# A macaron decoder layer on one core: the feed-forwards' exchange transfers issued by GpSimd, and one PSUM bank for the last quarter of the second down product

## The chip, the core and the metric

The kernel runs on one core of a Trainium2 chip, in one launch. The metric is the device time of a run in microseconds (us); three runs of the kernel before are known, and one more execution was taken with the hardware profiler. Engines are named as in the profile: PE is TensorE's matmul, PEld its weight load, DVE is VectorE, ACT is ScalarE, POOL is GpSimd, SP is SyncE, which here only issues transfers.

## The reference

One decoder layer on 256 tokens of width 1024, all in float32:

```python
h = h + 0.5 * swiglu(rms_norm(h, ffn1_norm), ffn1_w_gate, ffn1_w_up, ffn1_w_down)
h = h + hybrid_mixer(rms_norm(h, mix_norm), ...)     # two kinds of attention, gated, merged
h = h + 0.5 * swiglu(rms_norm(h, ffn2_norm), ffn2_w_gate, ffn2_w_up, ffn2_w_down)
out = rms_norm(h, final_norm)

def swiglu(x, w_gate, w_up, w_down):
    return (jax.nn.silu(x @ w_gate) * (x @ w_up)) @ w_down     # 1024 -> 2816 -> 1024
```

The change touches the two feed-forwards (swiglu) only.

## The kernel before

**Arithmetic.** Every product of float32 matrices is made of three matmuls on high and low parts: `mm3` issues a_high x w_high, a_high x w_low and a_low x w_high into one PSUM accumulation (lines 287, 288, 289). `unit` is one `mm3`, one step of the weave and one chance to prepare a weight tile.

**Weights.** All weights lie in HBM as one stream of 376 tiles of 128 x 512, in the order of their use. SP loads them in chunks of two tiles (512 KB, line 144) into three `raw` buffers; a chunk is issued when the third chunk before it has been split up. `Weights.split` makes a tile's parts: ACT writes the high part (`wh`, line 158 with the norm's gain, 155 without), DVE the low part (`wl`, line 159 or 156). `pump` lets this run up to 7 tiles ahead of the tile in use, in ten buffers.

**Order of the work.** PE and SP run in the order in which the program is written. For ACT, DVE and POOL a planner, which simulates the program at build time, sets the order of instructions, but for the first blocks of the first feed-forward and the end of the second one, where the written order holds (`ordered`). The weave is a list of generators: a generator that yields n goes on after n more units. So a constant such as `D_MOVED` sets where in the written order a step is put.

**A feed-forward** (`ffn`). The hidden width of 2816 is taken in 11 blocks b of 256. A block has 8 weight tiles, each with gate and up columns side by side, and two tiles t of 128 tokens: 16 units. After each of the two, `hidden` makes silu (ACT, line 397), the product (DVE, line 398) and a DVE transpose of 32 x 32 squares into `hs` (line 406). The transpose leaves each square in its place in the 4 x 4 grid, so `exchange` moves square (i, j) to (j, i) by 16 transfers from SBUF to SBUF (line 421, `hm` <- `hs`), one written after each unit, on SP's queue, for two blocks at once (six exchanges in a feed-forward, the last for one block). 14 steps behind, `split` makes the high and low parts `hth`, `htl` of the result (lines 308, 309), which the down product takes as its stationary side.

**The down product** goes over 22 rows k of 128 of the hidden width, two halves c of the output columns and two token tiles t, into four PSUM accumulations. The first 18 rows (the head) run with all four in turn; the last four (`TAIL`) are taken by one (t, c) after the other, so that each half is ready as early as it can be. In the second feed-forward the quarter (t, c) = (1, 1) is kept in two pieces of 256 columns in two PSUM banks over all 22 rows, so that the final norm can begin on the first piece while the second is still being accumulated. `residual` (line 486) adds half of a bank to h.

Other work on POOL: constants and a norm's Newton steps at the beginning, the same steps after the first feed-forward, rotary and mask work in the mixer, four transfers `bg` (line 834) and one `gB` (line 917).

The first feed-forward also carries `rope_tables` (lines 535 to 589), a chain of small DVE instructions for the rotary tables, which enters the weave at unit 100.

Of the kernel before, what the change touches and what calls it, by code (L numbers as in the profile page):

```python
# [23 lines left out]
KF = FF // P  # L24
# [11 lines left out]
WB = 10  # L36

D_TURNED = 3
D_MOVED = 14
D_TURN = 10  # L40
D_READY = 7
D_NORM0 = 9
# [141 lines left out]
def hybrid_layer_kernel(ctx, tc, x, xt, pos, g_final, bgate, wstream, out):  # L184
    nc = tc.nc
# [9 lines left out]
    def acc_bank(nm):  # L195
        return psum.tile([P, 512], F32, name=nm, tag="acc", bufs=3)

    def y_bank(nm):
        return psum.tile([P, 512], F32, name=nm, tag="y", bufs=1)

    def two_banks(nm):
        return psum.tile([P, 1024], F32, name=nm, tag="pr", bufs=2)

    def big(nm, dt=F32R):
        return work.tile([P, 1024], dt, name=nm, tag="big", bufs=24)

    def wide(nm, w=768):
        return work.tile([P, w], F32, name=nm, tag="f", bufs=4)
# [76 lines left out]
    def mm3(o, ah, al, w, first, last):  # L285
        wh, wl = w
        nc.tensor.matmul(o, ah, wh, start=first, stop=False)  # L287
        nc.tensor.matmul(o, ah, wl, start=False, stop=False)  # L288
        nc.tensor.matmul(o, al, wh, start=False, stop=last)  # L289

    def unit(o, a, w, first, last):
        mm3(o, a[0], a[1], w, first, last)
        weave.tick()
        W.pump()

    def unit_pair(os, blocks, w, first, last):

        wh, wl = w
        for o, (ah, al) in zip(os, blocks):
            nc.tensor.matmul(o, ah, wh, start=first, stop=False)  # L300
            nc.tensor.matmul(o, al, wh, start=False, stop=False)
        for o, (ah, al) in zip(os, blocks):
            nc.tensor.matmul(o, ah, wl, start=False, stop=last)
            weave.tick()
            W.pump()

    def split(dst_h, dst_l, src, hi_engine=None, rest=nc.vector):
        (hi_engine or nc.scalar.copy)(dst_h, src)
        rest.tensor_sub(dst_l, src, dst_h.bitcast(F32))
# [66 lines left out]
    def lagged(n, lag):  # L376

        for k in range(n + lag):
            if k < n:
                yield 0, k  # L380
            if k >= lag:
                yield 1, k - lag


    def ffn(base, xn, nm, on_half, lag, last=False):


        hts = {}
        squares = {}

        def slots(q):

            return q.rearrange("p (s w) -> p s w", w=P)

        def hidden(b, t, bank):
            sh = wide(f"sh_{nm}{b}_{t}", 512)
            silu = nc.scalar.activation(sh[:, 0:256], bank[:, 0:256], AF.Silu, scale=xn[t].r)
            prod = nc.vector.scalar_tensor_tensor(sh[:, 256:512], bank[:, 256:512], xn[t].r, sh[:, 0:256],
                                                  op0=ALU.mult, op1=ALU.mult)
            marks["silu"], marks["prod"] = silu.ins, prod.ins  # L400

            p = b // 2
            if p not in squares:
                squares[p] = big(f"hs_{nm}{b}", F32)
            dst = slots(squares[p])[:, b % 2 * 4 + t:b % 2 * 4 + t + 3:2]
            nc.vector.transpose(dst, sh[:, 256:512].rearrange("p (c w) -> p c w", w=P))
            if t == 1 and (b % 2 or b == FB - 1):
                weave.add(exchange(p, b % 2 * 4 + 4), D_TURNED)

        def later(f, *args):  # L410
            f(*args)
            return
            yield

        def exchange(p, n):

            moved = big(f"hm_{nm}{p}", F32)
            w = 32
            for i in range(4):
                for j in range(4):  # L420
                    nc.sync.dma_start(slots(moved)[j * w:j * w + w, 0:n, i * w:i * w + w],  # L421
                                      slots(squares[p])[i * w:i * w + w, 0:n, j * w:j * w + w])
                    yield 1
            yield D_MOVED
            hts[p] = big(f"hth_{nm}{p}"), big(f"htl_{nm}{p}")
            split(hts[p][0][:, 0:n * P], hts[p][1][:, 0:n * P], moved[:, 0:n * P])

        for b in range(FB):
            if b == 1:
                W.ahead = AHEAD  # L430
            if b == 2:
                ordered.close()
            banks = {}
            if b == 0 and lag == 0:
                pair = two_banks(f"gu_{nm}0")
                banks = {t: pair[:, t * 512:t * 512 + 512] for t in range(2)}
                for k in range(KD):
                    unit_pair([banks[t] for t in range(2)], [xn[t].blk(k) for t in range(2)], W.get(base + k),
                              k == 0, k == KD - 1)
                    W.done(base + k)  # L440
                for t in range(2):
                    weave.add(later(hidden, b, t, banks[t]), D_FIRST[t])
            for t, k in lagged(KD, 2 if b else lag) if b or lag else ():
                if k == 0:
                    banks[t] = acc_bank(f"gu_{nm}{b}_{t}")
                i = base + b * KD + k
                unit(banks[t], xn[t].blk(k), W.get(i), k == 0, k == KD - 1)
                if t == 1:
                    W.done(i)
                if k == KD - 1:  # L450
                    weave.add(later(hidden, b, t, banks[t]), 0 if b else D_FIRST[t])

        base += FB * KD
        banks = {}

        def out_bank(t, c):
            if (t, c) not in banks:
                if (t, c) != (1, 1):
                    banks[t, c] = acc_bank(f"dn_{nm}{t}{c}")
                else:  # L460
                    banks[t, c] = y_bank(f"dn_{nm}{t}{c}")
                    if last:
                        banks[t, c] = banks[t, c], two_banks(f"dn_{nm}{t}{c}b")
            return banks[t, c]

        def down(t, c, k, i, piece=None):

            o = k % 4 * 256 + t * P
            ht = [q[:, o:o + P] for q in hts[k // 4]]
            w = W.get(i)  # L470
            bank = out_bank(t, c)
            if (t, c) == (1, 1) and last:
                for j in range(2) if piece is None else (piece,):
                    mm3(bank[j][:, 0:256], *ht, [q[:, j * 256:j * 256 + 256] for q in w], k == 0, k == KF - 1)
                weave.tick()
                W.pump()
            else:
                unit(bank, ht, w, k == 0, k == KF - 1)

        def residual(t, c, piece=None):  # L480
            if piece is None:
                ps, s = banks[t, c][:, 0:512], slice(c * 512, c * 512 + 512)
            else:
                ps = banks[t, c][piece][:, 0:256]
                s = slice(c * 512 + piece * 256, c * 512 + piece * 256 + 256)
            nc.vector.scalar_tensor_tensor(h[t][:, s], ps, 0.5, h[t][:, s], op0=ALU.mult, op1=ALU.add)

        head = KF - TAIL
        for k in range(head):
            for c in range(2):  # L490
                for t in range(2):
                    down(t, c, k, base + 2 * k + c)
                W.done(base + 2 * k + c)
        weave.flush()
        if last:
            ordered.enter_context(tc.manual_schedule())
        for t in range(2):
            for c in range(2):
                pieces = (0, 1) if last and (t, c) == (1, 1) else (None,)
                for piece in pieces:  # L500
                    for k in range(head, KF):
                        i = base + 2 * head + c * TAIL + k - head
                        down(t, c, k, i, piece)
                        if t == 1 and piece in (None, 1):
                            W.done(i)
                    residual(t, c, piece)
                    on_half(t, c, piece)
# [87 lines left out]
    def next_norm(dst, nm):  # L595
# [12 lines left out]
        return on_half  # L608

    ffn(0, xn, "f1", next_norm(un, "u"), 0)  # L610
    with tc.issue_after(marks["silu"]):
        nc.scalar.preload_act_table_set("natural_log_exp_and_others")
# [192 lines left out]
    a, b, ys = {}, {}, {}  # L805
# [47 lines left out]
    for c in range(2):  # L853
        banks = {}
        for t, k in lagged(4, 2):
            if k == 0:
                banks[t] = acc_bank(f"ba{t}{c}")
            i = W_BR + c * 4 + k
# [28 lines left out]
    for t in range(2):  # L887
        for c in range(2):
            ps = acc_bank(f"bb{t}{c}")
            for k in range(4):  # L890
                i = W_BR + 8 + c * 4 + k
# [8 lines left out]
    for c in range(2):  # L900
        s = slice(c * 512, c * 512 + 512)
        for t in range(2):
            if (t, c) == (1, 0):
                weave.flush()
            ps = acc_bank(f"wo{t}{c}")
            for k in range(KD):
                i = W_OUT + c * KD + k
# [100 lines left out]
```

## Time and profile before

| | |
|---|---|
| median of 3 runs | 571.09 us (569.05 to 572.18) |
| the profiled execution | 569.89 us, of which span 568.0 us |
| mean granted TensorE clock | 0.994 |
| busy share of the span | PE 98%, PEld 80%, DVE 70%, ACT 60%, POOL 8% |
| chain that ended last | PE 84%, DMA 7%, DVE 4%, ACT 2% |

The span runs from the first to the last instruction of the execution. Busy shares count instructions, not waits or issues of transfers; the chain of work that ended last is followed back from the last instruction to what released each step.

### The profile page before, as it was taken

To read this page: it belongs to the slowest core of one execution; us is meant where nothing else is said; L and a number is where in the kernel's file an instruction comes from. 1 tells how busy PE (TensorE), PEld (TensorE's weight loads), DVE (VectorE), ACT (ScalarE), POOL (GpSimd) and SP (SyncE) were. 2 spreads that over 40 slices of the span, in tenths; PEclk is the share of its full clock that TensorE was granted. 3 is DMA by queue.
4 is the path that set the end of the run, shared out by engine and by line. 5 is a ranking of instruction groups with operands and counts; after the bars stand their busy time and mean duration, and the time that the engine had idled before them with its cause. 6 is when DMAs were issued, how large, how long until landed. Compare 5 with 4: busy or idle time off the path is not lost.

```text
span 568.0 us, 7807 instructions
## 1 busy us (share of the span) xinstructions
PE 555.2 (98%) x2580; PEld 456.2 (80%) x2580; DVE 395.0 (70%) x685; ACT 338.3 (60%) x576; POOL 43.5 (8%) x93
## 2 busy tenths in 40 slices
PE   9999989999999999999999999999999999999995
PEld 5778868778888888888888888788888878788884
DVE  6777595866466766879897878766667757754655
ACT  6855454755355666767867755466555655553643
POOL 1200000000000436000021200040000000000000
PEclk9999989999999999999999999999999999999998
DMA  8946757867687466433544564555667777786741
GB/s 299 399 101 202 188 176 194 231 194 202 171 292 255 148 199 217 159 137 112 185 134 162 185 198 148 181 176 188 181 191 213 213 203 206 206 194 195 248 156 74
DMA packets 78007, 109.57 MB, mean 193 GB/s; under 512 B 51600, under 2 KB 51856, under 8 KB 77968
## 3 DMA queue, kind: packets, MB, share of 16 engines
q1 hardware_dynamic: 77072, 106.85, 61.4%
q0 software_dynamic: 464, 1.57, 0.8%
q10 hardware_dynamic: 432, 0.67, 0.3%
q8 instruction: 20, 0.33, 0.2%
q14 instruction: 19, 0.16, 0.1%
HBM read 102.25 MB, written 1.05 MB: 182 GB/s over the span
## 4 chain that ended last, share of the span: by engine, by line
PE 84%; DMA 7%; DVE 4%; ACT 2%; issue 1%; SPq 1%; ACTq 0%
PE gu_f L288 11%; PE gu_f L289 10%; PE gu_f L287 10%; PE dn_f L287 7%; PE dn_f L288 7%; PE dn_f L289 7%; DMA raw<-in_wstream 6%; PE in L287 6%; PE in L288 6%; PE in L289 6%; DVE wl L159 2%; PE wo L287 1%; PE wo L289 1%; PE wo L288 1%; SPq L421 1%
## 5 line engine op out<-in xcount | busy, mean ns | idle before, releaser
L158 ACT ACTIVATE wh<-raw,first 128x512 fp32r<-128x512 f32 x256 | 173.6, 718 | 81.8 <-DMA raw<-in_wstream 51.5
L159 DVE SCALAR_TENSOR_TENSOR wl<-raw,first,wh 128x512 fp32r<-128x512 f32 x256 | 182.8, 748 | 56.2 <-ACT wh L158 55.5
L156 DVE TENSOR_TENSOR wl<-raw,wh 128x512 fp32r<-128x512 f32 x120 | 78.4, 690 | 43.9 <-ACT wh L155 43.5
L155 ACT CAST wh<-raw 128x512 fp32r<-128x512 f32 x120 | 69.5, 619 | 60.6 <-DMA raw<-in_wstream 43.9
L288 PE MATMUL gu_f<-wl,zh 128*128 128x512 f32 x176 | 68.7, 390 | 1.0 <-DVE wl L159 1.0
L287 PE MATMUL gu_f<-wh,zh 128*128 128x512 f32 x176 | 68.7, 391 | 0.0
L289 PE MATMUL gu_f<-wh,zl 128*128 128x512 f32 x176 | 68.5, 389 | 0.0
L288 PE MATMUL gu_f<-wl,xh 128*128 128x512 f32 x160 | 63.5, 397 | 3.2 <-DVE wl L159 2.9
L287 PE MATMUL dn_f<-wh,hth_f 128*128 128x512 f32 (+1 forms) x176 | 66.5, 378 | 0.0
L288 PE MATMUL dn_f<-wl,hth_f 128*128 128x512 f32 (+1 forms) x176 | 66.3, 377 | 0.0
L289 PE MATMUL dn_f<-wh,htl_f 128*128 128x512 f32 (+1 forms) x176 | 66.2, 376 | 0.0
L287 PE MATMUL in<-wh,uh 128*128 128x512 f32 x160 | 63.8, 399 | 0.0
L287 PE MATMUL gu_f<-wh,xh 128*128 128x512 f32 x160 | 63.5, 397 | 0.2 <-ACT wh L158 0.2
L289 PE MATMUL gu_f<-wh,xl 128*128 128x512 f32 x160 | 62.8, 393 | 0.0
L289 PE MATMUL in<-wh,ul 128*128 128x512 f32 x160 | 62.5, 391 | 0.0
L288 PE MATMUL in<-wl,uh 128*128 128x512 f32 x160 | 62.5, 391 | 0.0
L288 PEld LDWEIGHTS gu_f<-wl,zh 128*128 128x128 f32 x176 | 33.0, 188 | 8.4 <-DVE wl L159 1.7
L288 PEld LDWEIGHTS gu_f<-wl,xh 128*128 128x128 f32 x160 | 30.4, 190 | 10.8 <-DVE wl L159 3.9
L287 PEld LDWEIGHTS gu_f<-wh,zh 128*128 128x128 f32 x176 | 33.0, 188 | 7.3 <-ACT wh L158 0.5
L289 PEld LDWEIGHTS gu_f<-wh,zl 128*128 128x128 f32 x176 | 33.0, 188 | 6.8
L287 PEld LDWEIGHTS dn_f<-wh,hth_f 128*128 128x128 f32 x176 | 33.1, 188 | 6.4
L289 PEld LDWEIGHTS dn_f<-wh,htl_f 128*128 128x128 f32 x176 | 33.1, 188 | 6.2
(239 smaller groups left out, 755.7 us busy)
## 6 DMA issues: line engine op xcount, KB each, us to landing
raw<-in_wstream SPq DMA_DIRECT2D x184, 512.0 KB, 4.2
hm_f<-hs_f SPq DMA_DIRECT2D x160, 32.0 KB, 3.6
raw<-in_wstream SPq DMA_DIRECT2D x8, 256.0 KB, 5.4
h<-in_x SPq DMA_DIRECT2D x2, 512.0 KB, 6.7
bg<-in_bgate POOLq DMA_DIRECT2D x4, 256.0 KB, 3.9
xin<-in_xt SPq DMA_DIRECT2D x3, 256.0 KB, 5.6
hm_f<-hs_f SPq DMA_DIRECT2D x32, 16.0 KB, 2.9
gB<-in_g_final POOLq DMA_DIRECT2D x1, 512.0 KB, 5.1
```

What stands on the lines that cost most here:

```text
L155: self.nc.scalar.copy(hi, raw)
L156: self.nc.vector.tensor_sub(lo, raw, hi.bitcast(F32))
L158: self.nc.scalar.activation(hi, raw, AF.Copy, scale=g)
L159: self.nc.vector.scalar_tensor_tensor(lo, raw, g, hi.bitcast(F32), op0=ALU.mult, op1=ALU.subtract)
L287: nc.tensor.matmul(o, ah, wh, start=first, stop=False)
L288: nc.tensor.matmul(o, ah, wl, start=False, stop=False)
L289: nc.tensor.matmul(o, al, wh, start=False, stop=last)
L421: nc.sync.dma_start(slots(moved)[j * w:j * w + w, 0:n, i * w:i * w + w], slots(squares[p])[i * w:i * w + w, 0:n, j * w:j * w + w])
```

## The change

The 16 transfers of an exchange are issued by GpSimd in place of SyncE, and the generator that writes them yields 2 after each in place of 1; the wait behind the last one goes from 14 to 12 steps, so that the split is written 47 steps after the exchange has entered the weave's list, where it was 33. In the second feed-forward's down product, the head's 18 rows of quarter (1, 1) are accumulated by matmuls of 512 columns in one bank; its last four rows go, in two pieces of 256 columns, into two banks of their own, and a further `residual` adds the head's part.

```diff
-D_MOVED = 14
+D_MOVE = 2
+D_MOVED = 12
...
-                    nc.sync.dma_start(slots(moved)[j * w:j * w + w, 0:n, i * w:i * w + w],
-                                      slots(squares[p])[i * w:i * w + w, 0:n, j * w:j * w + w])
-                    yield 1
+                    nc.gpsimd.dma_start(slots(moved)[j * w:j * w + w, 0:n, i * w:i * w + w],
+                                        slots(squares[p])[i * w:i * w + w, 0:n, j * w:j * w + w])
+                    yield D_MOVE
             yield D_MOVED
...
                     banks[t, c] = y_bank(f"dn_{nm}{t}{c}")
-                    if last:
-                        banks[t, c] = banks[t, c], two_banks(f"dn_{nm}{t}{c}b")
...
-            bank = out_bank(t, c)
-            if (t, c) == (1, 1) and last:
-                for j in range(2) if piece is None else (piece,):
-                    mm3(bank[j][:, 0:256], *ht, [q[:, j * 256:j * 256 + 256] for q in w], k == 0, k == KF - 1)
+            if piece is not None:
+                if k == head:
+                    banks[piece] = two_banks(f"dn_{nm}p{piece}")
+                cols = slice(piece * 256, piece * 256 + 256)
+                mm3(banks[piece][:, 0:256], *ht, [q[:, cols] for q in w], k == head, k == KF - 1)
                 weave.tick()
                 W.pump()
             else:
-                unit(bank, ht, w, k == 0, k == KF - 1)
+                unit(out_bank(t, c), ht, w, k == 0, k == (head - 1 if last and (t, c) == (1, 1) else KF - 1))
...
-                ps = banks[t, c][piece][:, 0:256]
+                ps = banks[piece][:, 0:256]
...
         if last:
             ordered.enter_context(tc.manual_schedule())
+
+            residual(1, 1)
         for t in range(2):
```

## Rows read from the trace of the kernel before

**Rows 1.** Stretches with and behind an exchange: PE, PEld, DVE, ACT, POOL busy, clock, DMA share, GB/s.
```profile
57.00:71.00 14.00, 14.00 (x64) 11.58 (x63) 7.91 (x14) 6.23 (x11) 0.00 (x0) 1.00 0.78 191
71.00:83.00 12.00, 10.16 (x40) 7.95 (x39) 10.96 (x39) 6.87 (x11) 0.00 (x0) 0.89 0.49 171
```

**Rows 2.** PE's waits: us in total, times, longest us.
```profile
PE gu_f L288 <- DVE wl L159: 3.9, 5, 1.8
```

**Rows 3.** Timeline of PE around 100 us: start, us, what, [idle before].
```profile
99.71 0.48 PE L287 MATMUL gu_f<-wh,xh 128*128 128x512 f32 x1
100.72 0.50 PE L288 MATMUL gu_f<-wl,xh 128*128 128x512 f32 x1 [0.52 <-DVE wl L159]
```

**Rows 4.** Timeline of PE from 68 to 84 us.
```profile
68.04 0.39 PE L287 MATMUL gu_f<-wh,xh 128*128 128x512 f32 x1
...
76.88 0.39 PE L287 MATMUL gu_f<-wh,xh 128*128 128x512 f32 x1
79.11 0.50 PE L288 MATMUL gu_f<-wl,xh 128*128 128x512 f32 x1 [1.84 <-DVE wl L159]
...
80.39 0.56 PE L287 MATMUL gu_f<-wh,xh 128*128 128x512 f32 x1
...
84.03 0.40 PE L287 MATMUL gu_f<-wh,xh 128*128 128x512 f32 x1
```

**Rows 5.** Timeline of SP's queue, second exchange of the first feed-forward.
```profile
61.45 0.54 SPq L144 DMA_DIRECT2D raw<-in_wstream  x1
...
65.33 0.53 SPq L144 DMA_DIRECT2D raw<-in_wstream  x1
...
69.58 0.54 SPq L144 DMA_DIRECT2D raw<-in_wstream  x1
```

**Rows 6.** Timeline of ACT from 70 to 76 us.
```profile
70.96 0.47 ACT L397 ACTIVATE sh_f<-gu_f,r_x 128x256 f32<-128x256 f32 x1 [3.11 <-PE gu_f L289]
71.33 1.32 ACT L158 ACTIVATE wh<-raw,first 128x512 fp32r<-128x512 f32 x2
...
75.05 1.03 ACT L308 CAST hth_f<-hm_f 128x1024 fp32r<-128x1024 f32 x1
```

**Rows 7.** Timeline of DVE from 52 to 80 us.
```profile
52.27 0.45 DVE L406 STREAM_TRANSPOSE hs_f<-sh_f 128x256 f32<-128x256 f32 x1
...
74.53 0.61 DVE L542 TENSOR_SCALAR ang<-pf 128x2 f32<-128x2 f32 x8
...
78.31 1.41 DVE L159 SCALAR_TENSOR_TENSOR wl<-raw,first,wh 128x512 fp32r<-128x512 f32 x2
```

**Rows 8.** Transfers by line: engine, count, KB each, median us from issue to landing.
```profile
raw<-in_wstream SPq DMA_DIRECT2D x184, 512.0 KB, 4.2
hm_f<-hs_f SPq DMA_DIRECT2D x160, 32.0 KB, 3.6
...
bg<-in_bgate POOLq DMA_DIRECT2D x4, 256.0 KB, 3.9
```

**Rows 9.** Tile `hm_f`: duration ns min/median/max of an issue on SP.
```profile
L421 SPq DMA_DIRECT2D hm_f<-hs_f x192: 585/604/1772, 34.2 to 521.3; - x192
```

**Rows 10.** POOL's groups: busy us, mean ns of one, idle before.
```profile
L834 POOL DMA_DIRECT2D bg<-in_bgate x4 | 2.5, 616 | 8.8 <-DVE gate L840 8.7
...
L638 POOL TENSOR_TENSOR t_ka<-ka,sin 128x64 f32<-128x64 f32 x2 | 1.1, 552 | 0.0
...
L638 POOL TENSOR_TENSOR t_qa<-qa,sin 128x64 f32<-128x64 f32 x2 | 0.6, 321 | 0.0
```

**Rows 11.** Timeline of PE, one row k of the second down product's head.
```profile
547.42 0.40 PE L287 MATMUL dn_f<-wh,hth_f 128*128 128x512 f32 x1
...
549.49 0.28 PE L287 MATMUL dn_f<-wh,hth_f 128*128 128x256 f32 x1
...
550.20 0.40 PE L287 MATMUL dn_f<-wh,hth_f 128*128 128x512 f32 x1
```

**Rows 12.** Timeline at the end: a residual addition of 512 columns.
```profile
555.87 0.69 DVE L486 SCALAR_TENSOR_TENSOR h<-dn_f,h 128x512 f32<-128x512 f32 x1 [2.03 <-PE dn_f L289]
```

## The prediction, made before the changed kernel was built or run

> **What bounds the kernel now.** I read the shares first: PE is busy for 98% of the span and carries most of the chain that ended last, so time can only come from what PE waits for, from a slower clock, or from work taken off PE. PE's waits come next. Apart from the start there is one kind of any size: five waits of the gate and up products for a low part `wl`, 3.9 us together, the longest 1.8 [rows 2]. The other four are about 0.52 each ((3.9 - 1.84) / 4).
>
> The timeline of PE gives their true price, since a matmul's shown duration overlaps the next. Undisturbed, 39 matmuls of 512 columns take 8.84 us from 68.04 to 76.88, 0.2267 each [rows 4]. At a small wait the starts lie 1.01 apart [rows 3], a loss of 1.01 - 0.23 = 0.8. At the large one they lie 2.23 apart, a loss of 2.0, and behind it comes a second loss: from 80.39 to 84.03 nine matmuls take 3.64 where 9 x 0.2267 = 2.04 would do, so 1.6 more [rows 4]. That is the clock: the stretch behind this exchange shows a mean granted clock of 0.89, the one before it 1.00 [rows 1]. PE fell to the lower of its two levels (1.2 GHz for 2.4) shortly after it had stood idle. Together: 4 x 0.8 + 2.0 + 1.6 = 6.8 us. The two waits shown stand right behind the second and third exchanges of the first feed-forward; the other three too stand right behind an exchange.
>
> Why there? SP's queue says so. A chunk of two tiles lasts PE 2 x 6 x 0.2267 = 2.72 us, but during an exchange the chunks are issued at 61.45, 65.33 and 69.58, 3.9 and 4.25 apart [rows 5], because four or five exchange transfers, 0.604 each in the median and up to 1.77 [rows 9], stand between them. ACT then idles and the planner has put the silu, which must wait for PE, ahead of the weight tiles behind the late chunks: at 70.96 ACT has waited 3.11 us for PE, and the tiles follow at 71.33 [rows 6]. In the large case DVE has also put the rotary tables' small instructions, from 74.53 on, ahead of the next `wl`, at 78.31 [rows 7].
>
> **The exchange on GpSimd.** Removed from SP: 16 issues of 0.604 = 9.7 us per exchange, of some 14 us in which SP then has only three to five chunks of 0.54 to issue [rows 5, 9]. Chunks can go out as soon as their buffer is free, in the program's run as in the planner's simulation, from which the orders of ACT and DVE come. What I count is the end of the five stalls, 6.8 us at most and nothing at least.
>
> Added to POOL: 192 issues. The nearest price is that of `bg`, 0.616 us for a transfer of 128 rows [rows 10]. An exchange transfer has 32 rows with 8 pieces each, 256 pieces; no row shows such a transfer from POOL. Lower bound: as `bg`, 0.62. Upper bound: twice it, 1.23, plus what POOL's instructions lose beside DVE: one form takes 0.321 in one place and 0.552 on average in another [rows 10], 0.23 more, so 1.5. I take 0.9, nearer to the lower bound, because the row includes all that does not grow with the pieces. An exchange then lasts 16 x 0.9 = 14.4 us on a queue that has nothing else to do in the feed-forwards; what waits behind these transfers on POOL is the Newton steps of the next norm and, in the mixer, rotary and mask work, all later. Landing is 3.6 us from SP and 3.9 for `bg`, eight times as large [rows 8]; I take 4 to 5.
>
> The split of the exchanged tile, which ACT and DVE would hold up their queues for, moves from 33 to 47 steps behind: for the second exchange, whose last transpose starts at 52.27 [rows 7], from 75.05 [rows 6] to about 52.3 + 47 x 0.68 = 84.3 us (a unit is three matmuls, 0.68). POOL would be done at about 53 + 14.4 + 5 = 72.4, 12 us ahead. The last exchange is needed from row 20 of the down product on; its split is written 47 units into that product, and row 20 comes 72 units in or later. So I cost the later split at nothing; its cover is these 12 us, and at 1.5 us an issue it shrinks to 2.
>
> A rule speaks against the gain. The Trainium skill (DMA: Bandwidth & Descriptors, section Issuing engines are not separate DMA queues) says that transfers of all issuing engines share the same 16 DMA engines, so that spreading them saves only the time of issue, usually small. If nothing but a small issue time were saved, the bank's 1.1 below would be the whole gain, 570.0 (the second rival). The rows lean the other way: SP's issue time is not small, 9.7 of an exchange's 14 us [rows 1, 9], and it stands in front of the weights.
>
> **The quarter in one bank.** In the head a row k takes 550.20 - 547.42 = 2.78 us, of which six matmuls of 256 columns take 0.71 [rows 11]. With twelve of 512 it would be 12 x 0.2267 = 2.72. Saved: 0.06 x 18 = 1.1 us, on PE, which bounds this stretch (least 0.5, if only the six against three count: (0.71 - 0.68) x 18). The tail keeps its 24 matmuls of 256. Added: one `residual` of 0.69 us on DVE [rows 12] when the head ends. Behind it in the written order stands the `wl` of the last tail tile, which PE uses some seven units, 4.8 us, later; cost nothing. If that cover were gone it would cost its 0.69. Banks: the quarter gives back one of the two-bank buffers during the head, and takes both for the tail, when nobody else wants one.
>
> **Sum.** 6.8 + 1.1 = 7.9 of the profiled execution's 569.89, which makes 562.0. That execution was 1.2 us faster than the median of the three runs; against the median, 571.09 - 7.9 = 563.2.
>
> **The rivals.**
>
> *The rotary block still stalls (a partial gain).* The large wait had a second cause, the rotary tables on DVE, and the planner may again put them in one piece ahead of a `wl`. Then 3.6 of the 6.8 stay, and the gain is 3.2 + 1.1 = 4.3: 566.8. For: the instructions are many and short, from 74.53 to 78.31. Against: they went ahead when the weights were late, and the split that stood beside them moves some 9 us later.
>
> *The change does not do what it says.* The stalls have another cause, such as the order of silu and weight tiles at block ends, which a planner can repeat whatever SP does; only the bank's 1.1 is left: 570.0. For: twelve exchanges cause only five waits, so a late chunk alone is not enough. Against: none of the five stands away from an exchange.
>
> *The weights come late through the DMA engines.* SP spread an exchange over 14 us; POOL may put it out in 16 x 0.62 = 10, in one piece beside the weights, with a DMA share of 0.78 rising towards 1 [rows 1]. If a chunk is late once per exchange and costs a wait of 0.8, the ten full and two half exchanges cost some 11 x 0.8 = 8.8 in place of 6.8: 571.09 + 2.0 - 1.1 = 572.0. It decides when landing rises from 4.2 [rows 8] to about 6, since three chunks in flight last 8.2 us, of which the split takes some 2.1.
>
> *POOL cannot keep up (slower).* The place is the end of the down product. From the first exchange to the use of the last one PE has 9 blocks of 16 units, 18 rows of 4 and 2 units, 218 x 0.68 = 148 us; less 4 for landing and 2 for the split (1.03 on ACT [rows 6], about as much on DVE), 142 are left for 6 x 16 = 96 issues. So an issue of over 142 / 96 = 1.5 us makes PE wait, 9.6 us for each 0.1 more, in each feed-forward. At 1.6: 571.09 - 7.9 + 2 x 9.6 = 582. My upper bound, 1.5, stops just there. The Trainium skill (SBUF: State Buffer, section SBUF: two separate sides) holds that GpSimd cannot write a transfer's descriptors while DVE runs an instruction in a two-port mode. No row shows POOL issuing beside such an instruction; If each issue first waited for a whole `wl`, 1.41 / 2 = 0.7 us [rows 7], it would take 0.9 + 0.7 = 1.6, the case just priced; `bg` with its 0.616 was issued while DVE was busy too, in the mixer, which speaks against it.
>
> **How the numbers follow.** All five stalls gone, 563.2: 0.47. Rotary block stays, 566.8: 0.24. Only the bank, 570.0: 0.13. Late through the DMA engines, 572.0: 0.08. POOL's backlog, 574 and more, 582 at 1.6: 0.08. What can be told from no change is about 0.5% here, 2.9 us: the three runs lie 3.1 apart. So faster (under 568.2) is 0.47 + 0.24 and a little of the third case, 0.73; same is what is left of that and the fourth, 0.18; slower 0.09. The range runs from 561.0 (every small wait costs 0.1 more in slow matmuls behind it, and the runs lie at the profiled execution's level) to 570.0, which takes in the third case.
>
> **What the profile after would show.** SP's queue: chunks in the exchanges 2.7 to 2.9 apart, no line 421. POOL: 192 issues of 0.6 to 1.5 us, some 170 us busy in all. PE: no wait of the gate and up products for `wl`, and a granted clock of 1.00 behind the second exchange. ACT: `hth` split without a wait for `hm`. Second down product: a row k in 2.72, 18 rows in 49.0. It is wrong if waits for `wl` stay in number, if `hth` waits for `hm`, or if an issue on POOL takes over 1.5 us.

## The result, and the profile after

The changed kernel takes 562.82 us (median of 4 runs, 562.75 to 562.96), the kernel before 570.07 in the same comparison (4 runs, 568.66 to 572.18): 7.25 us less, a ratio of 0.987 with a 95% interval of 0.9835 to 0.9905. The forecast was 563.2.

PE's waits of the kernel after (us in total, times, longest us) answer to [rows 2]:

```profile
PE dn_f L288 <- DVE sh_f L399: 1.2, 2, 0.6
PE warm L279 <- DVE zeros L258: 1.1, 1, 1.1
PE gu_f L301 <- ACT wh L159: 0.4, 1, 0.4
PE tp_z L348 <- DVE h L913: 0.3, 1, 0.3
PE gu_f L289 <- DVE v_x L323: 0.3, 1, 0.3
```

The five waits of the gate and up products for `wl`, 3.9 us, are gone. Two waits are new: at the start of each down product PE waits 0.6 us for a product that DVE makes.

The two stretches of [rows 1] in the kernel after (PE, PEld, DVE, ACT, POOL busy, clock, DMA share, GB/s):

```profile
57.00:71.00 14.00, 14.00 (x63) 11.61 (x62) 10.03 (x16) 9.17 (x15) 5.99 (x11) 1.00 0.72 216
71.00:83.00 12.00, 12.00 (x54) 9.93 (x54) 11.59 (x43) 7.25 (x13) 7.13 (x13) 1.00 0.69 210
```

In the second one PE was busy for 10.16 of 12 us at a mean granted clock of 0.89; now it is busy throughout, at 1.00. Rotary tables and weight tiles both fit in: DVE is busy for 11.59 us.

SP's queue over the second exchange, to be set against [rows 5]:

```profile
46.51 43.23 SPq L145 DMA_DIRECT2D raw<-in_wstream  x17
```

Nothing but chunks: 17 issues in 43.23 us, 2.7 apart on average, PE's own pace. POOL's queue in the same stretch:

```profile
53.80 9.18 POOL L422 DMA_DIRECT2D hm_f<-hs_f  x16 [7.97 <-DVE hs_f L407]
75.86 7.47 POOL L422 DMA_DIRECT2D hm_f<-hs_f  x13 [12.88 <-issue]
85.02 1.73 POOL L422 DMA_DIRECT2D hm_f<-hs_f  x3 [1.69 <-DMA hm_f<-hs_f]
```

An exchange is put out in 9 to 11 us, right behind its transposes, and POOL then rests for 13. (Before the last three transfers of the later exchange here POOL stood idle for 1.7 us; the row names the landing of an earlier transfer.) Price and landing of an issue, from the tile's instructions and the page's transfers, answer to [rows 9] and [rows 8]:

```profile
L422 POOL DMA_DIRECT2D hm_f<-hs_f x192: 548/582/794, 34.5 to 505.5; - x192
```

```profile
raw<-in_wstream SPq DMA_DIRECT2D x184, 512.0 KB, 3.9
hm_f<-hs_f POOLq DMA_DIRECT2D x160, 32.0 KB, 3.7
```

Who waited for whom on ACT (us in total, times, longest us), before:

```profile
ACT wh L158 <- DMA raw<-in_wstream: 51.5, 37, 4.5
ACT wh L155 <- DMA raw<-in_wstream: 43.9, 33, 2.3
```

and after:

```profile
ACT wh L159 <- PE gu_f L290: 57.7, 88, 1.6
...
ACT wh L159 <- DMA raw<-in_wstream: 12.1, 10, 2.2
...
ACT hth_f L309 <- DMA hm_f<-hs_f: 5.2, 4, 2.1
...
ACT wh L156 <- DMA raw<-in_wstream: 2.0, 4, 0.9
```

For the tiles with the norm's gain (line 158, now 159) ACT's wait for chunks has shrunk from 51.5 us in 37 waits to 12.1 in 10, for the others from 43.9 to 2.0. What ACT now waits for is PE, 88 times, 0.66 us on average: a tile's buffer to come free. Loads and splits run as far ahead as the buffers let them.

The wait of `hth` for `hm` is one that the prediction had as a sign of being wrong. It is that of the last two exchanges of each feed-forward, whose splits ACT meets in the down product, for example:

```profile
143.12 0.62 ACT L309 CAST hth_f<-hm_f 128x512 fp32r<-128x512 f32 x1 [2.07 <-DMA hm_f<-hs_f]
```

PE, whose waits are all listed above, never waited for it.

In the second down product the head's row k lasts four units of 0.68 (timeline of PE, starts of the `wh` matmul of successive units; compare [rows 11]):

```profile
539.92 0.39 PE L288 MATMUL dn_f<-wh,hth_f 128*128 128x512 f32 x1
540.60 0.39 PE L288 MATMUL dn_f<-wh,hth_f 128*128 128x512 f32 x1
541.28 0.39 PE L288 MATMUL dn_f<-wh,hth_f 128*128 128x512 f32 x1
541.96 0.39 PE L288 MATMUL dn_f<-wh,hth_f 128*128 128x512 f32 x1
542.64 0.39 PE L288 MATMUL dn_f<-wh,hth_f 128*128 128x512 f32 x1
```

That is 2.72 us a row, where it was 2.78.

### The profile page after: what moved, and what is told of

Its sections match the earlier page's. It is cut to its first block, busy times and chain, and to the rows that moved or that the text cites. A ratio compares the mean times of both kernels' runs of the same rounds, so it can differ in the third digit from the quotient of the medians.

```text
span 561.1 us, 7756 instructions
## 1 busy us (share of the span) xinstructions
PE 551.1 (98%) x2526; PEld 452.9 (81%) x2526; DVE 397.5 (71%) x686; ACT 346.9 (62%) x576; POOL 153.1 (27%) x285
## 2 busy tenths in 40 slices
DMA packets 36026, 109.60 MB, mean 195 GB/s; under 512 B 6544, under 2 KB 7312, under 8 KB 35984
## 3 DMA queue, kind: packets, MB, share of 16 engines
q1 hardware_dynamic: 28944, 101.07, 54.9%
q0 software_dynamic: 6608, 7.35, 5.5%
## 4 chain that ended last, share of the span: by engine, by line
PE 90%; DMA 4%; POOL 2%; ACT 1%; DVE 1%; issue 1%; ACTq 0%
PE gu_f L289 12%; PE gu_f L288 12%; PE gu_f L290 12%; PE dn_f L288 7%; PE dn_f L290 7%; PE dn_f L289 7%; PE in L288 6%; PE in L290 6%; PE in L289 6%; DMA raw<-in_wstream 2%; POOL hm_f L422 2%; PE wo L290 1%; PE wo L288 1%; PE wo L289 1%; DMA hm_f<-hs_f 1%
## 5 line engine op out<-in xcount | busy, mean ns | idle before, releaser
L159 ACT ACTIVATE wh<-raw,first 128x512 fp32r<-128x512 f32 x256 | 179.4, 722 | 97.6 <-PE gu_f L290 57.7
L160 DVE SCALAR_TENSOR_TENSOR wl<-raw,first,wh 128x512 fp32r<-128x512 f32 x256 | 186.7, 748 | 67.1 <-ACT wh L159 66.8
L422 POOL DMA_DIRECT2D hm_f<-hs_f x192 | 109.7, 579 | 135.9 <-DVE hs_f L407 54.4
L157 DVE TENSOR_TENSOR wl<-raw,wh 128x512 fp32r<-128x512 f32 x120 | 81.4, 690 | 44.6 <-ACT wh L156 44.4
L156 ACT CAST wh<-raw 128x512 fp32r<-128x512 f32 x120 | 73.5, 622 | 62.8 <-DVE wl L157 42.4
L288 PE MATMUL dn_f<-wh,hth_f 128*128 128x512 f32 x172 | 67.3, 391 | 1.2 <-DVE sh_f L399 1.2
L290 PE MATMUL dn_f<-wh,htl_f 128*128 128x512 f32 x172 | 66.9, 389 | 0.0
L289 PE MATMUL dn_f<-wl,hth_f 128*128 128x512 f32 x172 | 66.9, 389 | 0.0
```

Source lines behind the costliest of these rows:

```text
L156: self.nc.scalar.copy(hi, raw)
L157: self.nc.vector.tensor_sub(lo, raw, hi.bitcast(F32))
L159: self.nc.scalar.activation(hi, raw, AF.Copy, scale=g)
L160: self.nc.vector.scalar_tensor_tensor(lo, raw, g, hi.bitcast(F32), op0=ALU.mult, op1=ALU.subtract)
L422: nc.gpsimd.dma_start(slots(moved)[j * w:j * w + w, 0:n, i * w:i * w + w], slots(squares[p])[i * w:i * w + w, 0:n, j * w:j * w + w])
```

## The experiments

Each kernel was compared with runs of the kernel before on the same chip, whose median is given beside it. The steps behind an exchange's entry at which its split is written are called its place: 33 in the kernel before, 47 in the changed one.

**The two parts alone.** `e1_pool_only` is the kernel before with the exchange part of the diff and nothing else.

> The exchange transfers on GpSimd with 2 and 12 steps, the second down product as before. Theory (the queue is what matters): the five waits for wl go, 6.8 us, of which the two new waits at the starts of the down products (0.6 us each in the profile after) take back 1.2 to 1.8, so 5 to 6 us faster than the kernel before, and 1.1 us slower than the changed kernel. Rival (the bank gives more than its 1.1): only 3 to 4 us faster.

Measured: 563.96 us (563.66 to 564.48) against 569.60, 0.9897 (0.9872 to 0.9923), so 5.6 us. The two new waits of 0.6 us are there, those for `wl` are not. This part carries most of the gain.

`e2_bank_only` is the changed kernel with this taken back:

```diff
-D_MOVE = 2
-D_MOVED = 12
+D_MOVED = 14
...
-                    nc.gpsimd.dma_start(...)
-                    yield D_MOVE
+                    nc.sync.dma_start(...)
+                    yield 1
```

> Only the bank layout of the second down product changes; exchange on SyncE with 1 and 14 steps. Theory: 0.5 to 1.1 us faster than before, a row k of the head 2.72 us, the five waits for wl and the slower clock behind the second exchange still there. Rival (bank and exchange help each other): 0, with the head's rows as slow as before.

Measured: 568.80 (567.47 to 569.88) against 569.60, 0.9984 (0.9968 to 1.0000), so 0.8 us, at the edge of what can be told. A row of the head is 2.72 us, and PE's waits are the old ones:

```profile
PE gu_f L288 <- DVE wl L159: 3.9, 5, 1.8
```

The parts alone give 5.6 + 0.8 = 6.4 of the 7.25; the intervals are wide enough to cover the rest.

**Spacing or queue?** `e3_sp_every_second` takes the steps of the change but leaves the transfers on SP (the kernel before otherwise).

```diff
-D_MOVED = 14
+D_MOVE = 2
+D_MOVED = 12
...
-                    yield 1
+                    yield D_MOVE
```

> The kernel before with the exchange still on SyncE, but one transfer every second step, and 12 steps behind the last. Rival to the theory (it is the spacing that matters, not the queue): two transfers of 0.6 us between two chunks leave SyncE time, chunks come 2.7 to 2.9 us apart, the waits for wl go, and it is 5 to 6 us faster. Theory (the queue matters): the transfers still stand in front of the chunks and the planner still sees them late; some waits for wl stay and less than half of the gain, at most 3 us, comes.

Measured: 567.32 (566.97 to 568.15) against 569.60, 0.9960 (0.9948 to 0.9973), 2.3 us. Four small waits for `wl` stay, 1.6 us in all; the large one is gone. On SP's queue chunks are still up to 3.7 us apart during the second exchange. `e1_pool_only` has the same steps and the same place and differs from this kernel in the queue alone: 563.96 against 567.32, 3.4 us. So the queue counts for more than the spacing, but the spacing and the later place alone bring some 40% of the exchange's gain.

`e12_sp_split_41` moves only the place, on SP, from 33 to 41 (`D_MOVED = 22` in the kernel before).

> The kernel before with 22 steps behind the last transfer, still one transfer per step on SyncE: only the split moves, to 41 steps. Theory (the queue matters): the five waits for wl stay, within 1 us of the kernel before. Rival (the moved split is what the change gives): 4 us or more faster.

Measured: 575.84 (574.05 to 576.63) against 569.45, 1.0102 (1.0073 to 1.0131): slower by 6.4 us, which neither expected. PE's waits:

```profile
PE gu_f L288 <- DVE wl L159: 4.2, 6, 1.8
PE dn_f L287 <- DVE sh_f L398: 3.0, 2, 1.6
...
PE gu_f L287 <- DVE sh_f L398: 1.0, 2, 0.6
```

The waits for `wl` stay, and waits for DVE's products come on top. So moving the split does not by itself bring the gain. But the place of the split is no free choice either.

**The place of the split, on GpSimd.** Four kernels are the changed one with other steps: `e4_pool_33` has 1 and 14 (place 33), `e8_pool_every_step_47` 1 and 28 (place 47), `e9_pool_41` 2 and 6 (place 41), `e10_pool_55` 2 and 20 (place 55). The edit of the third:

```diff
 D_MOVE = 2
-D_MOVED = 12
+D_MOVED = 6
```

> The changed kernel with one transfer per step and 14 steps, so that the split stands 33 steps behind as in the kernel before. If the new waits at the starts of the down products (0.6 us each) come from the split that now falls beside the last silu and product, they go here, and the time is 1.2 to 1.8 us below that of the changed kernel, 561 to 561.6. Rival (the later split is needed as cover for GpSimd's issue and landing): hth waits for hm and the time rises by 1 us or more.

Measured: 568.58 (564.59 to 571.79) against 569.60, 0.9975 (0.9946 to 1.0004). Nearly the whole gain is lost, and the runs scatter over 7 us. ACT's and PE's waits name the path:

```profile
ACT hth_f L309 <- DMA hm_f<-hs_f: 8.9, 6, 2.3
```

```profile
PE gu_f L288 <- DVE sh_f L399: 3.1, 2, 1.7
PE dn_f L288 <- DVE sh_f L399: 1.8, 1, 1.8
```

In the first feed-forward the planner has put the split's ACT instruction ahead of a block's silu; on the chip it waits there up to 2.3 us for the exchange to land, the silu and the product behind it are late, and PE waits for the PSUM bank that they free. ACT's timeline shows one such place:

```profile
50.67 1.05 ACT L309 CAST hth_f<-hm_f 128x1024 fp32r<-128x1024 f32 x1 [2.28 <-DMA hm_f<-hs_f]
52.86 0.45 ACT L398 ACTIVATE sh_f<-gu_f,r_x 128x256 f32<-128x256 f32 x1
```

That is the path of two of the three PE waits, 3.1 us. The third, 1.8 us, is another: in front of the silu at 133.39 ACT had waited 2.1 and 1.2 us for weight chunks to land. Why they came late there was not followed further.

> The changed kernel with a transfer written at every step and 28 steps behind the last: the split stands 47 steps behind, as in the changed kernel, the transfers twice as close in the written order. Theory (the split's place is what cost e4 its time: it was put ahead of the silu and waited for hm): as the changed kernel, 562.3 to 563.5. Rival (transfers written close together are bad on GpSimd too): as e4, 566 or more.

Measured: 562.96 (562.50 to 563.19) against 570.11, 0.9874 (0.9859 to 0.9889): the changed kernel's time. On GpSimd the spacing of the transfers makes no difference that shows; what cost `e4_pool_33` its time goes with the place of the split.

> The changed kernel with 6 steps behind the last transfer, so that the split stands 41 steps behind, in the middle of a block and not beside its last product. Theory: the two waits of the down products for DVE's product (0.6 us each, 1.2 to 1.8 with the slow matmuls behind them) go, hth still finds hm landed; 561.0 to 561.6. Rival (the earlier split waits for hm, as with 33 steps): 564 or more.

Measured: 561.10 (561.06 to 561.17) against 570.11, 0.9842 (0.9828 to 0.9857). It beats both kernels: 9.0 us less than before. No wait of a down product for DVE is left:

```profile
PE warm L279 <- DVE zeros L258: 1.0, 1, 1.0
PE tp_z L348 <- DVE h L913: 0.3, 1, 0.3
PE gu_f L289 <- DVE v_x L323: 0.3, 1, 0.3
```

So the new waits come from the place of the split. A block has 16 units, so 47 falls on the last unit but one of a block, and the low part `htl` runs ahead of the block's last product. In the changed kernel, DVE and PE at the end of the first feed-forward's last block:

```profile
127.50 1.23 DVE L310 TENSOR_TENSOR htl_f<-hm_f,hth_f 128x1024 fp32r<-128x1024 f32 x1 [0.17 <-DMA hm_f<-hs_f]
128.64 0.48 DVE L399 SCALAR_TENSOR_TENSOR sh_f<-gu_f,r_x,sh_f 128x256 f32<-128x256 f32 x1
```

```profile
128.18 0.39 PE L290 MATMUL dn_f<-wh,htl_f 128*128 128x512 f32 x1
129.17 0.50 PE L288 MATMUL dn_f<-wh,hth_f 128*128 128x512 f32 x1 [0.60 <-DVE sh_f L399]
```

(The row names a landing; the input that `htl` needed last was its `hth`, which ACT made from 126.42 to 127.47.) The third bank that the down product opens is one that the block's last product must free. With the split at 41, mid-block, the product starts at 127.77, where it started at 128.64, and PE does not wait.

> The changed kernel with 20 steps behind the last transfer: the split stands 55 steps behind, again in the middle of a block. If the place inside the block is what matters, as with 41 steps: 560.8 to 561.5, no wait of the down product for DVE's product. Rival (only an earlier split helps): as the changed kernel, 562.5 to 563.5.

Measured: 561.18 (560.92 to 561.34) against 569.45, 0.9847 (0.9831 to 0.9863), no such wait: as 41. On GpSimd a place in the middle of a block does the same, earlier or later; 33, at a block's start, fails for the other reason, the landing.

**The rotary tables.** `e7_sp_rope_late` is the kernel before with `weave.add(rope_tables(), 110)` in place of 100.

> The kernel before, with the rotary tables entering the weave 10 steps later, in the middle of a block. If the tables were what made the large wait (2.0 us and 1.6 at the slower clock), it shrinks to a wait like the other four, 0.8, and the time falls by 2 to 3 us. If the late chunks alone make it, the large wait stays in its place and the time is that of the kernel before within 1 us.

Measured: 569.46 (568.46 to 571.79) against 570.11, 0.9996 (0.9980 to 1.0011). It tells nothing: the tables hang on the product that was last written when they enter, which was still the same one, and they ran from 75.01 us on, in one piece ahead of a `wl` as before. `e7b_sp_rope_120` enters them at 120.

> The kernel before, with the rotary tables entering the weave at unit 120, behind the products of the block that ends at unit 112, so that they can't stand at 75 us. If the tables made the large wait, it shrinks to 0.5 us like the other four, the slower clock behind it goes, and the time falls by 2 to 3 us. If the late chunks alone make it, a wait of about 1.8 us stays near 79 us and the time is that of the kernel before within 1 us.

Measured: 566.17 (565.91 to 566.41) against 569.45, 0.9935 (0.9919 to 0.9951), 3.3 us. The tables now start at 86.80, and the large wait is gone with the slower clock (PE's waits, and the stretch of [rows 1] in this kernel):

```profile
PE gu_f L288 <- DVE wl L159: 2.1, 4, 0.5
```

```profile
71.00:83.00 12.00, 12.00 (x54) 9.94 (x53) 9.98 (x16) 8.73 (x14) 0.00 (x0) 1.00 0.75 246
```

So the large wait needed both: late chunks and a block of small instructions that was ready while the weight tiles were not. In the changed kernel the tables still start at 75.22, but `wl` instructions stand between them.

**GpSimd's limit.** `e5_pool_32_issues` and `e6_pool_64_issues` cut every transfer of the changed kernel in two and in four, by slots:

```diff
-                    nc.gpsimd.dma_start(slots(moved)[j * w:j * w + w, 0:n, i * w:i * w + w],
-                                        slots(squares[p])[i * w:i * w + w, 0:n, j * w:j * w + w])
+                    for o in range(4):
+                        s = slice(o * n // 4, (o + 1) * n // 4)
+                        nc.gpsimd.dma_start(slots(moved)[j * w:j * w + w, s, i * w:i * w + w],
+                                            slots(squares[p])[i * w:i * w + w, s, j * w:j * w + w])
                     yield D_MOVE
```

> The changed kernel with every transfer cut in two (half of the slots each): 32 issues per exchange. GpSimd's price if an issue costs the same whatever its pieces: 32 x 0.58 = 18.6 us per exchange, less than the 21.8 in which the next one becomes ready, no backlog, 562.3 to 564. If the price goes with the pieces, an issue takes 0.3 to 0.4 us and the time is that of the changed kernel. Rival (the cover is thin): splits wait for hm and the time rises by 2 us or more.

Measured: 562.76 (562.32 to 562.78) against 570.11, 0.9869 (0.9852 to 0.9885), with 0.548 us an issue: twice the issues cost nothing. (The cut has a side effect: the first half of the slots is ready a block earlier, and POOL's first issue stands at 28.7 us, where it stood at 34.5.)

> The changed kernel with every transfer cut in four: 64 issues per exchange. With 0.55 us per issue, as for transfers cut in two, an exchange takes 35 us of GpSimd, more than the 21.8 in which the next becomes ready. Theory of the backlog: 6 x 64 x 0.55 = 211 us against some 150 from the first exchange to the use of the last, so PE waits about 60 us in each feed-forward, 670 to 700 us in all. Rival (GpSimd is never in the way): below 575 us.

Measured: 690.79 (687.27 to 691.78) against 569.45, 1.2111 (1.2073 to 1.2149). An issue takes 0.533 us, an exchange of 64 then 34, more than the next one's 21.8; in the first feed-forward POOL issues almost without a pause from 28.7 to 241.6 us, and the down product waits for the splits:

```profile
PE dn_f L288 <- ACT hth_f L309: 89.8, 5, 35.8
PE gu_f L288 <- DVE sh_f L399: 10.1, 4, 4.3
PE dn_f L288 <- DVE sh_f L399: 7.3, 3, 3.8
```

The backlog is real, and it sets in somewhere between 17.5 and 34 us of POOL's time per exchange; the changed kernel uses 9 to 11.

## Why the prediction was right

**The five waits.** Forecast 6.8 us. The exchange part alone gives 5.6, with the two new waits in it. Taking those out, as `e9_pool_41` does, is worth 562.82 - 561.10 = 1.7, so the waits for `wl` and the slower clock cost about 5.6 + 1.7 = 7.3 us together. By `e9_pool_41` itself, 9.0 less the bank's 0.8, it is 8.2. Either is over the sum made from the timeline. Their path was read rightly, chunks late on SP's queue, then the planner's order: `e1_pool_only` against `e3_sp_every_second` shows the queue, `e7b_sp_rope_120` that the large wait had the rotary tables as a second cause, which the prediction held as a rival. In the changed kernel that rival did not come true: with chunks in time the tables and the `wl` stand mixed in DVE's order. How much of a wait is the late chunk itself, and how much the order that the planner made because of it, stays open; every kernel with another queue was also planned anew.

**The later split, costed at nothing.** This step failed. For the first four exchanges of a feed-forward the cover was there: no split of theirs waited for `hm`. But the cost lies in the place: written 47 steps behind, the split falls beside a block's last product and holds up a PSUM bank, 1.7 us over both feed-forwards. And some later place was needed: at 33, where the split waits for the landing of GpSimd's exchange, 568.58 - 562.82 = 5.8 us are lost in the median. The prediction treated the move as free; in truth it kept 5.8 us and gave back 1.7.

Its sign of being wrong, that `hth` waits for `hm`, did come up, four times in the last two exchanges, 5.2 us in all, and nothing was lost by it. ACT met the last split of the first feed-forward at 143.12, some 23 units into the down product and not the 47 at which it is written, since the planner sets ACT's order. In these runs a wait of the split could cost time where a silu stood behind it (`e4_pool_33`), and cost none where ACT only had weight tiles to prepare; that was not in the prediction.

That the time came within 0.4 us of the forecast is in part luck. The gain was 7.25 and not 7.9: the waits were worth 0.5 to 1.4 us more than forecast, the split's place took 1.7 and the bank gave 0.3 less. And the kernel before ran at 570.07 in this comparison, 1.0 below the 571.09 from which the forecast subtracts.

**The bank.** Forecast 1.1, measured 0.8 alone, with an interval that reaches from nothing to 1.8; the row of 2.72 us came as worked out. The added `residual` costs PE nothing that shows: no wait for it is listed.

**GpSimd's price.** Taken as 0.9, bounds 0.62 and 1.5; measured 0.582, below the lower bound. An issue hardly grows with the pieces of a transfer: 0.582 for 256 pieces, 0.548 for 128, 0.533 for 64 (medians of the three kernels; a sixth of the transfers have half as many pieces). Landing, taken as 4 to 5, was 3.7. The error cost nothing, since POOL had time to spare. The threshold of 1.5 us an issue, 24 an exchange, lies within what `e5` and `e6` bracket. No issue was held up by a DVE instruction to any length: the longest of 192 took 0.794, with DVE busy for 71% of the span. The Trainium skill (SBUF — State Buffer, section SBUF: two separate sides) has such a hold-up for DVE instructions in a two-port mode. No row tells which of DVE's instructions ran in that mode, so the runs don't speak against the rule.

**The sharing of the DMA engines.** The rival that the weights would come late did not occur; chunks land in 3.9 us instead of 4.2. Nor is that faster landing the cause of the gain: in `e9_pool_41`, the fastest kernel, they land in 4.2 as before. What was saved is the place in SP's queue. The Trainium skill (DMA: Bandwidth & Descriptors, section Issuing engines are not separate DMA queues) has it that another issuing engine saves only issue time, which is usually small beside the transfer itself. These runs agree with the first part. As to the second, one issue of 0.604 us is small beside its landing of 3.6, but sixteen are 9.7 us within 14, in front of a prefetch.

## What to carry to other kernels

When small transfers and a prefetch share an issuing queue, price the queue in its own time: issues times their duration in the stretch against the period of the prefetch, and look in the compute engines' order for what the planner did because it thought the prefetch late. After moving work, ask not only whether a later step is covered but which instruction of the same engine it now stands in front of; here six steps earlier or eight later were worth 1.7 us, and fourteen earlier cost 5.8. A PE wait is dearer than it reads: the five listed at 3.9 us cost 7 to 8.

## What was not expected of the hardware

A transfer of 256 pieces of 128 bytes makes far fewer packets when GpSimd issues it: the page counts 78,007 DMA packets before and 36,026 after. GpSimd's queue went from 464 to 6,608, so 32 for each of the 192 transfers; SP's fell from 77,072 to 28,944, so 251 for each on average (32 of the 192 have 128 pieces). The DMA share of the queues hardly moved, 61.4 + 0.8% before, 54.9 + 5.5% after (packets, MB, share; before, then after):

```profile
q1 hardware_dynamic: 77072, 106.85, 61.4%
q0 software_dynamic: 464, 1.57, 0.8%
```

```profile
q1 hardware_dynamic: 28944, 101.07, 54.9%
q0 software_dynamic: 6608, 7.35, 5.5%
```

The clock fell to its lower level behind the wait of 1.84 us, for some 3.6 us [rows 4], and not behind any of 0.5 to 0.6 us. It did not fall behind every longer one either: in `e4_pool_33` the granted clock stayed at 1.00 behind waits of 1.45, 1.70 and 1.76 us, while in `e12_sp_split_41` it was 0.50 from 80 to 83 us, behind one of 1.83 (PE in the two kernels):

```profile
134.66 0.50 PE L288 MATMUL dn_f<-wh,hth_f 128*128 128x512 f32 x1 [1.76 <-DVE sh_f L399]
```

```profile
79.45 0.50 PE L288 MATMUL gu_f<-wl,xh 128*128 128x512 f32 x1 [1.83 <-DVE wl L159]
```

The runs of the changed kernel lie closer together than those of the one before, 0.2 us apart against 3.5, and so do those of `e7b_sp_rope_120`, 0.5, which lacks the large wait only. That the large wait is what scatters them is not shown: `e4_pool_33` is without it and scatters over 7.2.
